# Gate and up of a SwiGLU layer: four of eight pairs of k-tiles as 2x2 blocks with seven products, and one shared set of large tiles

## Chip, cores and metric

The kernel runs on one core of a Trainium2 chip. The metric is the time of one execution on the device in microseconds, the median of three runs. Matrix products are TensorE's (PE), elementwise work is done by VectorE (DVE) and ScalarE (ACT), GpSimd (POOL) has a few small operations, and SyncE (SP) issues the loads.

## The reference

Two layers of a hybrid encoder over 256 positions with 2048 channels, all in float32. The part that the change touches is the last but one line of a layer:

```
for l in range(DEPTH):                                   # DEPTH = 2
    h = rmsnorm(x, norm1_g[l])
    proj = h @ w_in[l]                                   # q, k, v, uv
    a = dilated_attention(q, k, v)
    g = chunked_spatial_gating(uv, ...)
    x = x + concat(rmsnorm(a), rmsnorm(g)) @ w_out[l]
    h = rmsnorm(x, norm2_g[l])                           # 256 x 2048
    ff = silu(h @ w_gate[l]) * (h @ w_up[l])             # 2048 x 5632 each
    x = x + ff @ w_down[l]                               # 5632 x 2048
return rmsnorm(x, final_g)
```

## The kernel before

Every matrix product is made of three terms. A weight tile arrives as float32 ("raw"); ACT copies it to a shorter form ("hi", L646) and DVE subtracts that from the raw tile ("lo", L647). Activations are split in the same way. A product then takes three matmuls of 128x128 by 128x512 (TERMS, L699): hi by hi, hi by lo and lo by hi.

The weights come in 1 MB loads. One load is a **pair** of k-tiles (2 x 128 rows of the weight) by two column blocks of 512. A **group** (`_groups`) is one output of 256 rows by two such column blocks, so it fills four PSUM banks (two halves t of the rows, two blocks n). For gate and up, block n = 0 is 512 columns of gate and n = 1 the same 512 columns of up, and a group runs over 8 pairs: 8 x 24 = 192 matmuls. There are 11 such ff groups in a layer, in parts of FF_PARTS = (4, 4, 3); behind each part come two groups that apply the rows of w_down belonging to it.

When a group's last pair is done, ACT takes the gate banks (silu, L482), DVE multiplies them with the up banks (L485) into ffn, and a side task (`Ffn.turn`) transposes ffn on PE (tpf), and splits the result on ACT (L181) and DVE (L182) for the down groups.

The order is written by hand. One program loop goes over the pairs, in two **slots** of 12 matmuls each (t = 0, 1). In a slot it issues, in this order: the loads three pairs ahead (LA_DMA), the splits up to three slots ahead (LA_SPLIT), the slot's matmuls, the evacuations of banks that are complete (`done`), and up to two steps of side tasks (`run_side`). Each engine takes its own instructions strictly in the order in which they are issued, so an instruction that waits holds everything behind it on that engine. The tile pools have 4 raw, 4 hi and 4 lo tiles, PSUM has five banks for groups and three for side tasks.

Of the kernel before, what the change touches and what calls it, by code (L numbers as in the profile page):

```python
# [8 lines left out]
F32 = mybir.dt.float32  # L9
# [25 lines left out]
FF_PARTS = (4, 4, 3)  # L35
# [3 lines left out]
CH = 2 * NB  # L39
LA_DMA = 3  # L40
LA_SPLIT = 3
WARM = 4
TAIL = 2
# [10 lines left out]
def _groups():  # L54

    for l in range(DEPTH):
        seen = {}
        for what, ca, cb in W_IN:
            seen[what] = idx = seen.get(what, -1) + 1
            yield l, what, idx, 0, KD // 2, (("w_in", ca), ("w_in", cb))  # L60
        for what, row in (("oa", 0), ("og", DA)):
            for m in range(2):
                yield l, what, m, row, 4, (("w_out", 2 * m * NB), ("w_out", (2 * m + 1) * NB))
        j0 = 0
        for i, nj in enumerate(FF_PARTS):
            for m in range(j0, j0 + nj):
                yield l, "ff", m, 0, KD // 2, (("w_gate", m * NB), ("w_up", m * NB))
            for m in range(2):
                yield l, f"down{i}", m, j0 * NB, 2 * nj, (("w_down", 2 * m * NB), ("w_down", (2 * m + 1) * NB))
            j0 += nj  # L70


@with_exitstack
def encoder_kernel(ctx: ExitStack, tc: tile.TileContext, x, xf, w, ws, lng, cols, fg, cs, msk, out):
# [33 lines left out]
    mskt = cpool.tile([P, NT, SEQ], F32, name="mskt")  # L108

# [80 lines left out]

    def transposes(src, k, name):
# [14 lines left out]
    class Norm:  # L206


        def __init__(self, l, which):
            self.l, self.which = l, which  # L210
            self.ss = smp.tile([P, NT, D // NB], F32, tag="ssn", name=f"ssn_{which}_{l}", bufs=2)
            self.blocks = [KTiles(hpool, "h", f"h_{which}_{l}_{b}") for b in range(KD // KR)]
            self.n = 0
            self.rstd = None

# [10 lines left out]
        def block(self, b):  # L226

            for k in (0, 2):
                ps = transposes(xt[b], k, f"tpn_{self.which}_{self.l}_{b}_{k}")
                yield 1  # L230
                put_splits(self.blocks[b], k, ps, [gcol(self.l, self.which, b * KR + k + j) for j in range(2)])
# [3 lines left out]
        def early(self, b, k, src):  # L235

            put_split(self.blocks[b], k, src, gcol(self.l, self.which, b * KR + k))
# [11 lines left out]
        def lhs(self, k):  # L249
            force(lambda: self.blocks[k // KR].ready[k % KR])  # L250
            return self.blocks[k // KR], k % KR


    class Mixer:


        def __init__(self, l, norm):
# [9 lines left out]
            self.v = [None, None]  # L267
            self.u = [None, None]
# [3 lines left out]
        def load(self):  # L272
            l = self.l
            self.lng = s4p.tile([P, DG], F32, tag="s4", name=f"lng_{l}")
            self.ws = s4p.tile([P, NG, P], F32, tag="s4", name=f"ws_{l}")
# [4 lines left out]
        def value(self, t, half, ps):  # L280
            if self.v[half] is None:
                self.v[half] = mpool.tile([P, 2, NT, NB], F32R, tag="mf", name=f"v_{self.l}_{half}")
# [42 lines left out]
        def head(self, h):  # L325
# [11 lines left out]
            sm = s2p.tile([P, NT, SEQ], F32, tag="sm", name=f"sm_{l}_{h}")  # L337
# [22 lines left out]
            pT = s2p.tile([P, 2, NT, SEQ], F32R, tag="pT", name=f"pT_{l}_{h}")  # L360
# [4 lines left out]
            for c in range(NT):  # L365
                for n, (a, b) in enumerate(TERMS):
# [407 lines left out]
```

## Time and profile before

| | before |
|---|---|
| median of 3 runs | 2167.38 us (2167.27 to 2167.85) |
| profiled execution: its time | 2170.74 us |
| profiled execution: span from first to last instruction | 2168.9 us |
| mean granted TensorE clock | 0.997 |
| PE busy | 2138.9 us (99%) |
| DVE busy | 1169.3 us (54%) |
| ACT busy | 958.1 us (44%) |
| weight loads of 1 MB | 375 |

Busy time counts the instructions that compute, not waiting. A PE that is busy 99% of the span says only that it hardly ever waits; whether an engine with 54% has room at a certain place is read from a window, and how long its instructions take from their rows. All matmul rows print a duration of some 390 ns though they start 227 ns apart: they are pipelined, and the pace is the distance of their starts.

### The profile page before, as it was taken

The page shows a single profiled execution, that of the slowest core. Times are in us where ns is not written, and L with a number is a line of the kernel's source. Part 1 is how long each engine was busy: PE and PEld are TensorE (multiplying, and loading weights), DVE is VectorE, ACT ScalarE, POOL GpSimd, SP SyncE. Part 2 cuts the span into 40 slices and gives each one's busy share as a digit, 9 for nine tenths or more (in the row PEclk, how much of TensorE's full clock was granted, in tenths as well). Part 3 has the DMA queues.
Part 4 walks back from the last instruction along what each step waited for, and adds up shares of the span by engine and source line. Part 5 has one row for each costly group of instructions (what it writes and reads, how often), then busy time and mean ns, then how long its engine had stood idle before and what let it go on. Part 6 is the DMA issues. An engine that isn't in the chain of part 4 may idle for free.

```text
span 2168.9 us, 24017 instructions
## 1 busy us (share of the span) xinstructions
PE 2138.9 (99%) x9696; PEld 1770.0 (82%) x9696; DVE 1169.3 (54%) x1258; ACT 958.1 (44%) x1215; POOL 85.8 (4%) x64
## 2 busy tenths in 40 slices
PE   8999999999999999999999999999999999999997
PEld 6877888888888888888888788888888888888886
DVE  5577656445444444444556766554444454445445
ACT  5445545444334443344454555454433344333443
POOL 0121100000000000000002200000000000000000
PEclk9999999999999999999999999999999999999999
DMA  8444455555555555555555444555555555555552
GB/s 321 176 160 170 175 188 179 191 185 187 194 194 194 183 187 194 193 194 186 184 185 182 156 175 175 191 179 193 187 186 193 194 192 194 185 193 188 191 213 97
DMA packets 58800, 405.85 MB, mean 187 GB/s; under 512 B 6592, under 2 KB 6592, under 8 KB 10560
## 3 DMA queue, kind: packets, MB, share of 16 engines
q1 hardware_dynamic: 58688, 404.31, 51.9%
q8 instruction: 76, 1.25, 0.2%
q14 instruction: 36, 0.29, 0.0%
HBM read 402.19 MB, written 2.10 MB: 186 GB/s over the span
## 4 chain that ended last, share of the span: by engine, by line
PE 95%; DVE 2%; DMA 1%; issue 0%; ACT 0%; SPq 0%; POOL 0%; POOLq 0%; DVEq 0%; ACTq 0%
PE mm L699 92%; DVE lo L647 1%; PE tpf L196 1%; DVE rb_q L305 1%; DMA raw<-in_w 1%; PE sp L333 1%; PE op L367 1%; PE tpn_n L196 0%; DMA xf<-in_xf 0%; PE ptp L359 0%; PE mix L436 0%; DVE rb_k L305 0%; ACT hi L646 0%; PE tpg L196 0%; SPq L666 0%
## 5 line engine op out<-in xcount | busy, mean ns | idle before, releaser
L647 DVE TENSOR_TENSOR lo<-raw,hi 128x1024 fp32r<-128x1024 f32 (+1 forms) x754 | 904.5, 1226 | 930.9 <-ACT hi L646 928.4
L699 PE MATMUL mm<-hi,h_n 128*128 128x512 f32 x4096 | 1291.1, 392 | 7.9 <-ACT hi L646 5.0
L646 ACT ACTIVATE hi<-raw 128x1024 fp32r<-128x1024 f32 (+1 forms) x754 | 767.8, 1051 | 1050.9 <-PE mm L699 1028.5
L699 PEld LDWEIGHTS mm<-hi,h_n 128*128 128x128 f32 x4096 | 771.0, 188 | 167.6 <-ACT hi L646 6.2
L699 PE MATMUL mm<-lo,h_n 128*128 128x512 f32 x2048 | 800.7, 391 | 7.8 <-DVE lo L647 7.8
L699 PEld LDWEIGHTS mm<-lo,h_n 128*128 128x128 f32 x2048 | 385.8, 188 | 89.1 <-DVE lo L647 12.6
L699 PE MATMUL mm<-hi,ff 128*128 128x512 f32 x1408 | 438.9, 390 | 0.0
L699 PEld LDWEIGHTS mm<-hi,ff 128*128 128x128 f32 x1408 | 264.3, 188 | 54.6
L699 PE MATMUL mm<-lo,ff 128*128 128x512 f32 x704 | 274.0, 389 | 0.0
L699 PEld LDWEIGHTS mm<-lo,ff 128*128 128x128 f32 x704 | 132.2, 188 | 27.0
L699 PE MATMUL mm<-hi,a 128*128 128x512 f32 x256 | 84.1, 399 | 0.0
L699 PE MATMUL mm<-hi,g 128*128 128x512 f32 x256 | 81.3, 392 | 0.0
L699 PEld LDWEIGHTS mm<-hi,a 128*128 128x128 f32 x256 | 48.1, 188 | 10.0
L699 PEld LDWEIGHTS mm<-hi,g 128*128 128x128 f32 x256 | 48.1, 188 | 9.8
L699 PE MATMUL mm<-lo,a 128*128 128x512 f32 x128 | 49.9, 390 | 0.0
L699 PE MATMUL mm<-lo,g 128*128 128x512 f32 x128 | 49.9, 390 | 0.0
L203 POOL TENSOR_TENSOR rstd_n<-rstd_n,mhalf 128x2 f32<-128x2 f32 x4 | 2.8, 696 | 926.2 <-DVE rstd_n L202 926.2
L181 ACT ACTIVATE ff<-tpf 128x512 fp32r<-128x512 f32 x44 | 26.4, 600 | 29.0 <-PE tpf L196 27.6
L182 DVE TENSOR_TENSOR ff<-tpf,ff 128x512 fp32r<-128x512 f32 x44 | 30.2, 687 | 7.9 <-ACT ff L181 7.9
L485 DVE SCALAR_TENSOR_TENSOR ffn<-mm,rstd_n,sil 128x512 f32<-128x512 f32 x44 | 32.9, 747 | 1.6 <-ACT sil L482 1.3
L602 DVE TENSOR_TENSOR xt<-mm,xt 128x512 f32<-128x512 f32 x48 | 30.9, 681 | 4.0 <-PE mm L699 4.0
L346 ACT ACTIVATE sm<-sm,mx 128x256 f32<-128x256 f32 x32 | 16.0, 502 | 37.9 <-DVE mx L343 37.9
(103 smaller groups left out, 708.0 us busy)
## 6 DMA issues: line engine op xcount, KB each, us to landing
raw<-in_w SPq DMA_DIRECT2D x375, 1024.0 KB, 4.8
xt<-in_x SPq DMA_DIRECT2D x4, 512.0 KB, 13.6
out<-xt SPq DMA_DIRECT2D x8, 256.0 KB, 3.1
xf<-in_xf SPq DMA_DIRECT2D x3, 512.0 KB, 10.2
raw<-in_w SPq DMA_DIRECT2D x4, 256.0 KB, 6.5
ws<-in_ws SPq DMA_DIRECT2D x2, 512.0 KB, 3.6
lng<-in_lng SPq DMA_DIRECT2D x2, 512.0 KB, 5.4
fg<-in_fg SPq DMA_DIRECT2D x1, 1024.0 KB, 7.0
```

The lines of the kernel that those rows point to most:

```text
L181: nc.scalar.activation(out=hi, in_=src, func=AF.Copy)
L182: nc.vector.tensor_tensor(out=kt.t[:, k:k + 2, 1, :], in0=src, in1=hi.bitcast(F32), op=ALU.subtract)
L196: nc.tensor.transpose(ps[:, j, t, :], src[:, t, (k + j) * P:(k + j + 1) * P], ident)
L305: nc.vector.tensor_tensor(out=b[:, :, to], in0=s[:, :, of], in1=sin, op=ALU.mult)
L333: nc.tensor.matmul(sp[:, t, :], lhsT=q[:, a, i, t * P:(t + 1) * P], rhs=k[:, b, i, :], start=(n == 0), stop=(n == len(TERMS) - 1),)
L346: nc.scalar.activation(out=sm[:, t, :], in_=sm[:, t, :], func=AF.Exp, bias=mx[:, t:t + 1], accum_out=den[:, t:t + 1])
L367: nc.tensor.matmul(op, lhsT=v[:, a, c, f * HD:(f + 1) * HD], rhs=pT[:, b, c, :], start=(c == 0 and n == 0), stop=(c == NT - 1 and n == len ...
L485: nc.vector.scalar_tensor_tensor(out=self.ff[:, t, :], in0=ps, scalar=self.norm.scale(t), in1=self.silu, op0=ALU.mult, op1=ALU.mult)
L602: nc.vector.tensor_tensor(out=xb, in0=ps, in1=xb, op=ALU.add)
L646: nc.scalar.activation(out=hi[:, sl], in_=src[:, sl], func=AF.Copy)
L647: nc.vector.tensor_tensor(out=lo[:, sl], in0=src[:, sl], in1=hi[:, sl].bitcast(F32), op=ALU.subtract)
L699: nc.tensor.matmul(ps, lhsT=a.part(xl, ka, t), rhs=hl[kk][wl][:, n, :], start=(j == 0 and kk == 0 and z == 0), stop=(j == pairs - 1 and kk ...
```

## The change

The ff groups change their arithmetic. The first four of the eight pairs of a group ("fast") are taken as 2x2 blocks: A11 to A22 are the two row halves of the activations by the two k-tiles of a pair, B11 to B22 the two k-tiles by gate and up. Seven products give the four results (Strassen's scheme in Winograd's form). Each product M1 to M7 runs over the four fast pairs with three terms: 12 matmuls, one slot, into a bank. The weights' sums (T1 to T4) are made by DVE in place in the raw tiles q11, q12, q21, q22 of 128x2048 (`add`, L836), between the splits that need the earlier contents; the activations' sums (S1 to S4) are made once for a layer by `sums` (L252, L255, L256) when norm2's result is there. The other four pairs stay as they were, in two slots each. A group has 15 slots instead of 16, in the order of ORDER, or of FIRST for the first ff group of a layer.

Splits in ff groups are made of 2048 columns at once (L858 on ACT, L859 on DVE). M1 and M5 go to banks that ACT copies to SBUF (L913); DVE adds the products together (`finish`, L917 to L927) and silu (L623) and the multiplication (L626) read the SBUF sums. FF_PARTS becomes (3, 3, 3, 2). The separate pools of raw, hi, lo and other large tiles give way to one shared set of 17 tiles of 8 KB in each partition (`Big`). Loads are issued five slots ahead, splits two slots ahead in ff groups with an index above 0 and three elsewhere. The transposes for norm2 start earlier: `delay=1 + n, rank=0` instead of `delay=1 + 4 * n`.

```diff
-FF_PARTS = (4, 4, 3)
-CH = 2 * NB
-LA_DMA = 3
+FF_PARTS = (3, 3, 3, 2)
+FAST = {"ff": 4}
+BANK = {(0, 0): "v", (0, 1): "z", (1, 0): "x", (1, 1): "w"}
+PRODUCT = {
+    "M1": ("1", "A11", "B11"), "M2": ("v", "A12", "B21"), "M3": ("z", "S4", "B22"), "M4": ("x", "A22", "T4"),
+    "M5": ("5", "S1", "T1"), "M6": ("6", "S2", "T2"), "M7": ("7", "S3", "T3"),
+}
+ORDER = ("N", "M1", "N", "M5", "M2", "N", "M6", "M3", "M7", "M4", "N")
+FIRST = ("M1", "M5", "M2", "M6", "M3", "N", "M7", "N", "M4", "N", "N")
+LOADS = {"M1": ("q11", "q12"), "M5": ("q22",), "M2": ("q21",)}
+CH = 4 * NB
+N_BIG = 17
+LA_LOAD = 5
 LA_SPLIT = 3
...
+    def sums(raw, n, dst):
+        r = raw.view("p (j f q) -> p j f q", j=2, f=8)[:, :n]
+        f = lambda i: r[:, :, i, :]
+        for to, a, op, b in (
+            (3, f(7), ALU.subtract, f(2)), (4, f(3), ALU.subtract, f(0)),
+            (5, f(0), ALU.subtract, f(7)), (6, f(1), ALU.add, f(4)),
+        ):
+            nc.vector.tensor_tensor(out=f(to), in0=a, in1=b, op=op)
+        src = r[:, :, 0:7, :].rearrange("p j f q -> p j (f q)")
+        hi, lo = (dst.rearrange("p (j h z) -> p j h z", h=2, z=7 * P)[:, :, i] for i in range(2))
+        nc.scalar.activation(out=hi, in_=src, func=AF.Copy)
+        nc.vector.tensor_tensor(out=lo, in0=src, in1=hi.bitcast(F32), op=ALU.subtract)
...
             if what == "og" and t == NT - 1:
-                spawn(norms["n2", l].block(b), delay=1 + 4 * n)
+                spawn(norms["n2", l].block(b), delay=1 + n, rank=0)
...
+        def add(self, to, of):
+            cols = self.fast * NB
+            a, b = (self.raw[q].t[:, :cols] for q in (to, of))
+            nc.vector.tensor_tensor(out=a, in0=a, in1=b, op=ALU.add)
...
+        def split(self, key, pieces=1):
...
+                q = {"M1": "q11", "M5": "q11", "M6": "q11", "M2": "q21", "M4": "q21", "M7": "q12", "M3": "q22"}
...
+            if key == "M3":
+                self.add("q12", "q22")
...
+                nc.scalar.activation(out=hi[:, sl], in_=src[:, sl], func=AF.Copy)
+                nc.vector.tensor_tensor(out=lo[:, sl], in0=src[:, sl], in1=hi[:, sl].bitcast(F32), op=ALU.subtract)
...
+            if key == "M1":
+                self.add("q11", "q12")
+            elif key == "M5":
+                self.add("q11", "q22")
+            elif key == "M2":
+                self.add("q21", "q11")
...
+                b, f, _ = PRODUCT[m]
+                for p in range(self.fast):
+                    act = norms["n2", self.l].form(p)
+                    for z, (xl, wl) in enumerate(TERMS):
+                        mac(b, act(xl, f), hl[0][wl][:, p * NB:(p + 1) * NB],
+                            self.last[b] == i and p == self.fast - 1 and z == len(TERMS) - 1)
...
+        def finish(self, b):
+            ps, c = self.banks[b][0], self.copies
+            if b in "15":
+                c[b] = sx(f"m{b}_{self.g}")
+                nc.scalar.activation(out=c[b], in_=ps, func=AF.Copy)
+                return
+            if b == "6":
+                c["x"] = sx(f"m16_{self.g}")
+                nc.vector.tensor_tensor(out=c["x"], in0=ps, in1=c["1"], op=ALU.add)
+                c["z"] = sx(f"m5_16_{self.g}")
+                nc.vector.tensor_tensor(out=c["z"], in0=c["5"], in1=c["x"], op=ALU.subtract)
+                return
+            if b == "7":
+                nc.vector.tensor_tensor(out=c["x"], in0=ps, in1=c["x"], op=ALU.add)
+                nc.vector.tensor_tensor(out=c["5"], in0=c["5"], in1=c["x"], op=ALU.subtract)
+                c["v"], c["w"] = c["1"], c["5"]
+                return
+            if b in c:
+                nc.vector.tensor_tensor(out=c[b], in0=ps, in1=c[b], op=ALU.add)
+                ps = c[b]
+            t, n = next(k for k, v in BANK.items() if v == b)
+            done(self.l, self.what, self.idx, t, n, ps)
...
+    events = sorted(
+        [(s - LA_LOAD, 0, i) for i, (s, *_) in enumerate(loads) if i >= KD // KR]
+        + [(s - (2 if gr.fast and gr.idx else LA_SPLIT), 1, i) for i, (s, gr, _) in enumerate(splits)]
+    )
```

What stands in the engines' queues is told by the program, without times. The names are made of the group's number (9 is the first ff group of layer 0, 20 one in its third part) and the product or pair, and the last number only counts.

ACT's queue before, around the silu of an ff group (here gate block 8 of layer 0, group 21):

```order
L646 ACTIVATE hi_320_6567<-raw_160_6515 128x1024
L646 ACTIVATE hi_321_6585<-raw_160_6515 128x1024
L482 ACTIVATE sil_0_8_0_6596<-mm_21_0_0_6347,rstd_n2_0_2992 128x512
L646 ACTIVATE hi_322_6605<-raw_161_6549 128x1024
L482 ACTIVATE sil_0_8_1_6615<-mm_21_1_0_6365,rstd_n2_0_2992 128x512
L646 ACTIVATE hi_323_6627<-raw_161_6549 128x1024
```

ACT's queue after the change, at the start of group 20 (layer 0), behind the second silu of the group ahead:

```order
L623 ACTIVATE sil_0_6_1_5486<-m16_19_5398,rstd_n2_0_2816 128x512
L858 ACTIVATE hi_20_M1_5498<-raw_20_q11_5439 128x2048
L858 ACTIVATE hi_20_5_5519<-raw_20_5_5455 128x2048
L913 ACTIVATE m1_20_5552<-mm_20_1_5539 128x512
L858 ACTIVATE hi_20_M5_5554<-raw_20_q11_5439 128x2048
L858 ACTIVATE hi_20_M2_5572<-raw_20_q21_5517 128x2048
L234 ACTIVATE ff_0_6_5571<-tpf_0_6_0_5589 128x2x256
L858 ACTIVATE hi_20_6_5596<-raw_20_6_5537 128x2048
```

Before, only the silu stands between the splits of weights. After, the copy of M1's bank (m1) stands between hi 5 and hi M5, so everything behind it comes after M1's matmuls.

DVE's queue after the change, at the same place; q11, q12, q21, q22 are the raw tiles of the weight blocks:

```order
L927 TENSOR_TENSOR m5_19_5332<-mm_19_w_5251,m5_19_5332 128x512
L626 SCALAR_TENSOR_TENSOR ffn_0_6_5468<-m5_19_5332,rstd_n2_0_2816,sil_0_6_1_5486 128x512
L859 TENSOR_TENSOR lo_20_M1_5499<-raw_20_q11_5439,hi_20_M1_5498 128x2048
L836 TENSOR_TENSOR raw_20_q11_5439<-raw_20_q11_5439,raw_20_q12_5441 128x2048
L859 TENSOR_TENSOR lo_20_5_5520<-raw_20_5_5455,hi_20_5_5519 128x2048
L859 TENSOR_TENSOR lo_20_M5_5555<-raw_20_q11_5439,hi_20_M5_5554 128x2048
L836 TENSOR_TENSOR raw_20_q11_5439<-raw_20_q11_5439,raw_20_q22_5496 128x2048
L859 TENSOR_TENSOR lo_20_M2_5573<-raw_20_q21_5517,hi_20_M2_5572 128x2048
L836 TENSOR_TENSOR raw_20_q21_5517<-raw_20_q21_5517,raw_20_q11_5439 128x2048
L235 TENSOR_TENSOR ff_0_6_5571<-tpf_0_6_0_5589,ff_0_6_5571 128x2x256
L859 TENSOR_TENSOR lo_20_6_5597<-raw_20_6_5537,hi_20_6_5596 128x2048
```

Where the queue before has one lo part of 1024 columns for each slot, here lo parts and additions of 2048 columns alternate, and the lo part of pair 6, which PE needs in its eighth slot, stands behind four lo parts and three additions of its group.

DVE's queue after the change in the first ff group of layer 0; hr and h_n2 are the activations' sums and their split, xt the residual, to which L757 adds the product of w_out:

```order
L836 TENSOR_TENSOR raw_9_q11_2538<-raw_9_q11_2538,raw_9_q12_2540 128x2048
L252 TENSOR_TENSOR hr_n2_0_1_2513<-hr_n2_0_1_2513 128x2x128 x4
L256 TENSOR_TENSOR h_n2_0_2330<-hr_n2_0_1_2513,h_n2_0_2330 128x2x896
L859 TENSOR_TENSOR lo_9_M5_2619<-raw_9_q11_2538,hi_9_M5_2618 128x2048
L836 TENSOR_TENSOR raw_9_q11_2538<-raw_9_q11_2538,raw_9_q22_2567 128x2048
L757 SCALAR_TENSOR_TENSOR xt_2_99<-mm_8_v_2469,rstd_g_0_2290,xt_2_99 128x512
L757 SCALAR_TENSOR_TENSOR xt_3_100<-mm_8_z_2470,rstd_g_0_2290,xt_3_100 128x512
L859 TENSOR_TENSOR lo_9_M2_2642<-raw_9_q21_2589,hi_9_M2_2641 128x2048
L836 TENSOR_TENSOR raw_9_q21_2589<-raw_9_q21_2589,raw_9_q11_2538 128x2048
L757 SCALAR_TENSOR_TENSOR xt_2_99<-mm_8_x_2497,rstd_g_0_2290,xt_2_99 128x512
```

PE's queue at the same place, between M1 and M5 of that group:

```order
L880 MATMUL mm_9_1_2666<-hi_9_M1_2591,h_n2_0_2330 128x512 x2
L880 MATMUL mm_9_1_2666<-lo_9_M1_2592,h_n2_0_2330 128x512
L880 MATMUL mm_9_1_2666<-hi_9_M1_2591,h_n2_0_2330 128x512
L264 MATMUL tpn_n2_0_4_2681<-ident_81,xt_2_99 128x128 x4
L880 MATMUL mm_9_5_2691<-hi_9_M5_2618,h_n2_0_2330 128x512
L880 MATMUL mm_9_5_2691<-lo_9_M5_2619,h_n2_0_2330 128x512
```

The last addition into xt_2 stands behind two further lo parts and two block additions on DVE, and PE's transposes of xt_2 stand ahead of M5.

## Rows read from the trace of the kernel before

**Rows 1.** The page: span, busy time, chain that ended last, weight loads.

```profile
span 2168.9 us, 24017 instructions
...
PE 2138.9 (99%) x9696; PEld 1770.0 (82%) x9696; DVE 1169.3 (54%) x1258; ACT 958.1 (44%) x1215; POOL 85.8 (4%) x64
...
PE 95%; DVE 2%; DMA 1%; issue 0%; ACT 0%; SPq 0%; POOL 0%; POOLq 0%; DVEq 0%; ACTq 0%
...
raw<-in_w SPq DMA_DIRECT2D x375, 1024.0 KB, 4.8
```

**Rows 2.** Waits of PE: us in total, times, longest us.

```profile
PE mm L699 <- DVE lo L647: 7.8, 8, 1.3
```

**Rows 3.** Four ff groups: us; busy PE, PEld, DVE, ACT, POOL; PEclk; DMA; GB/s.

```profile
353.52:531.00 177.48, 177.48 (x804) 146.97 (x803) 89.85 (x91) 80.86 (x100) 0.69 (x1) 1.00 0.53 189
```

**Rows 4.** Timeline of PE in the ff groups: start us, us, operation.

```profile
443.18 0.62 PE L699 MATMUL mm<-hi,h_n 128*128 128x512 f32 x2
...
443.86 0.62 PE L699 MATMUL mm<-hi,h_n 128*128 128x512 f32 x2
...
446.13 0.60 PE L196 MATMUL tpf<-ident,ffn 128*128 128x128 f32 x4
...
490.60 0.60 PE L196 MATMUL tpf<-ident,ffn 128*128 128x128 f32 x4
```

**Rows 5.** Tiles hi and lo: duration ns min/median/max, first and last start.

```profile
L646 ACT ACTIVATE hi<-raw x754: 629/1058/1101, 7.1 to 2145.4; 128x1024 fp32r<-128x1024 f32 x188, 128x512 fp32r<-128x512 f32 x1
L647 DVE TENSOR_TENSOR lo<-raw,hi x754: 691/1224/2314, 7.8 to 2146.7; 128x1024 fp32r<-128x1024 f32 x188, 128x512 fp32r<-128x512 f32 x1
```

**Rows 6.** Timelines of DVE and ACT at four places.

```profile
715.98 0.68 DVE L182 TENSOR_TENSOR ff<-tpf,ff 128x512 fp32r<-128x512 f32 x1
716.58 1.21 DVE L647 TENSOR_TENSOR lo<-raw,hi 128x1024 fp32r<-128x1024 f32 x1
...
742.51 2.36 DVE L647 TENSOR_TENSOR lo<-raw,hi 128x1024 fp32r<-128x1024 f32 x2 [3.08 <-ACT hi L646]
...
741.42 2.01 ACT L646 ACTIVATE hi<-raw 128x1024 fp32r<-128x1024 f32 x2 [3.43 <-PE mm L699]
...
196.87 0.68 DVE L338 SCALAR_TENSOR_TENSOR sm<-sp,mskt 128x512 f32<-128x512 f32 x1
197.59 0.69 DVE L343 TENSOR_REDUCE mx<-sm 128x2 f32<-128x512 f32 x1
```

**Rows 7.** Groups of instructions: busy us, mean ns of one, idle before them.

```profile
L699 PE MATMUL mm<-hi,h_n 128*128 128x512 f32 x4096 | 1291.1, 392 | 7.9 <-ACT hi L646 5.0 <-ACT s_q L293 2.9
L482 ACT ACTIVATE sil<-mm,rstd_n 128x512 f32<-128x512 f32 x44 | 29.9, 679 | 0.6
L181 ACT ACTIVATE ff<-tpf 128x512 fp32r<-128x512 f32 x44 | 26.4, 600 | 29.0 <-PE tpf L196 27.6
L598 DVE SCALAR_TENSOR_TENSOR xt<-mm,rstd_g,xt 128x512 f32<-128x512 f32 x16 | 11.2, 743 | 0.0
L172 DVE SCALAR_TENSOR_TENSOR h_n<-tpn_n,colt,h_n 128x256 fp32r<-128x256 f32 x48 | 20.9, 476 | 0.0
```

**Rows 8.** Timeline of PE at the start.

```profile
7.83 0.80 PE L699 MATMUL mm<-hi,h_n 128*128 128x512 f32 x1 [4.40 <-ACT hi L646]
...
11.66 1.05 PE L699 MATMUL mm<-hi,h_n 128*128 128x512 f32 x2
12.52 0.63 PE L699 MATMUL mm<-lo,h_n 128*128 128x512 f32 x1
...
15.29 0.63 PE L699 MATMUL mm<-hi,h_n 128*128 128x512 f32 x2
```

**Rows 9.** Timeline of PE around a set of norm2's transposes.

```profile
350.34 0.60 PE L196 MATMUL tpn_n<-ident,xt 128*128 128x128 f32 x4
350.69 0.48 PE L699 MATMUL mm<-hi,g 128*128 128x512 f32 x1
```

**Rows 10.** Cores: span and mean granted TensorE clock.

```profile
core 0: 2168.9 us, clock 0.997
```

More of the change, by code (lines that the diff above doesn't have):

```diff
@@ L247, in scale, with normal, form @@
             return self.rstd[:, t:t + 1]
-        def lhs(self, k):
-            force(lambda: self.blocks[k // KR].ready[k % KR])
-            return self.blocks[k // KR], k % KR
+        def normal(self, p):
+            force(lambda: self.ready[p])
+            return lambda hl, kk, t: self.pairs[p].part(hl, kk, t)
+        def form(self, p):
+            force(lambda: self.ready[p])
+            return lambda hl, f: self.pairs[p][:, hl, FORMS[f], :]
     class Mixer:
@@ L457, in gating @@
                 return
+            for z in (self.gvb, self.lw, self.ub):
+                z.free()
             yield 1
@@ new lines, in encoder_kernel @@
+    groups = [Group(g, spec) for g, spec in enumerate(_groups())]
+    slots, loads, first_slot = [], [], {}
+    off = 0
+    for gr in groups:
+        first_slot[gr.g] = len(slots)
+        for key, width, i in gr.loads():
+            loads.append((first_slot[gr.g] + i, gr, key, width, off))
+            off += P * width
+        slots += [(gr, i) for i in range(len(gr.slots))]
+    splits, seen = [], set()
+    for s, (gr, i) in enumerate(slots):
+        for key in gr.chunks(gr.slots[i]):
+            if (gr.g, key) not in seen:
+                seen.add((gr.g, key))
+                splits.append((s, gr, key))
@@ new lines, in encoder_kernel, with next_event @@
+    events = sorted(
+        [(s - LA_LOAD, 0, i) for i, (s, *_) in enumerate(loads) if i >= KD // KR]
+        + [(s - (2 if gr.fast and gr.idx else LA_SPLIT), 1, i) for i, (s, gr, _) in enumerate(splits)]
+    )
+    pos = 0
+    def next_event(now, must):
+        nonlocal pos
+        if pos == len(events):
+            return False
+        when, kind, i = events[pos]
+        due = splits[i][0] if kind else loads[i][0]
+        if not must:
+            need = splits[i][1].need(splits[i][2]) if kind else 1
+            if count["live"] + need > N_BIG - reserve(now) or when > now:
+                return False
+        if kind:
+            _, gr, key = splits[i]
+            gr.split(key, pieces=2 if i < 2 else 1)
+        else:
+            _, gr, key, width, o = loads[i]
+            gr.load(key, width, o)
+        pos += 1
+        return True
@@ new lines, in reserve, with split_by @@
+    def reserve(now):
+        gr = slots[now][0]
+        return {"v": 1, "qk": 2, "gv": 1, "u": 1, "oa": 1, "og": 1, "ff": 1}.get(gr.what, 1)
+    def split_by(s):
+        while pos < len(events) and any(
+            (splits[i][0] if kind else loads[i][0]) <= s for _, kind, i in events[pos:pos + 12]
+        ):
+            assert next_event(s, True)
+    xf_b = [Big(f"xf_{b}") for b in range(2)]
+    xf_t = [xf_b[b // 2].view("p (b k q) -> p b k q", b=2, k=KR)[:, b % 2] for b in range(KD // KR)]
```

411 lines of the change are left out of this document (287 added, 124 removed).

## Prediction

> **What bounds the kernel now.** I read the head of the page first. TensorE (PE) is busy 99% of the span and 95% of the chain that ended last; VectorE (DVE) has 54% and ScalarE (ACT) 44% [rows 1]. The view of waits agrees: PE's longest sum of waits is 7.8 us for lo parts, in 8 waits of the whole span [rows 2]. In the first four feed-forward (ff) groups PE is busy 177.48 of 177.48 us while DVE works 89.85 and ACT 80.86 [rows 3]: half of DVE's time is free there. The timeline gives PE's pace: three matmuls in 0.68 us, 0.2267 each; the same transposes return after 490.60 - 446.13 = 44.47 us, which is one ff group: 192 matmuls (43.52) and 0.95 for its transposes [rows 4]. So what counts is whether the other engines can still feed PE once a group has fewer matmuls and more vector work.
>
> **What is removed.** A group in blocks has 180 matmuls: 15 slots of 12, each 2.72 us, so 40.80 + 0.95 = 41.75 us instead of 44.47. With 22 ff groups that is 264 x 0.2267 = 59.8 us, all on the path that sets the end, if nothing else comes up.
>
> **What is added on DVE and ACT.** Durations first. A lo part of 1024 columns takes 1.224 us and one of 512 takes 0.691, so 0.533 for each 512 more [rows 5]; back to back the second 1024 starts some 1.14 after the first, and an operation behind one of 512 starts 0.60 after it [rows 6]. For 2048 columns, which no row of before has, I estimate 2.29 us long and 2.20 from start to start; an addition of the same size reads and writes the same amounts, so it gets the same. Bounds: 2 x 1.22 = 2.44 above (nothing gained by the longer form) and 4 x 0.533 = 2.13 below (no fixed part). An operation that needs the result of the one just ahead starts 0.04 after its end instead of 0.09 before it [rows 6]. A hi part on ACT goes 0.629, 1.058, so 1.92 for 2048 [rows 5]. Additions of 512 columns cost 0.68 to 0.69 [rows 6], silu 0.68 and a copy of a bank on ACT 0.60 [rows 7]. A bank's sum is out 0.392 - 0.227 = 0.165 after the last matmul's turn [rows 4, 7]; with the hand-over I take 0.2, and 0.05 for other hand-overs, as between ACT's 741.42 + 1.06 and DVE's 742.51 [rows 6].
>
> Splits per group: before 16 of 1024 columns (18.2 us of DVE), now eleven of 2048, and four additions of 2048 (the sums of weight blocks): 15 x 2.20 = 33.0. About twelve operations of 512 (recombination, activation, transposed results) give 7.3, and seven waits for its own result 0.9: 41.2 us of DVE for 41.75 us of PE. That alone leaves 0.5 us of slack; the order of the queues takes it away. ACT has some 26 us of work and room.
>
> **A steady ff group** (7 of 11 in a layer), t = 0 at the end of the group before on PE. ACT's queue there reads silu, hi M1, hi 5, the copy of M1's bank, hi M5, hi M2. The silu ends at 0.28, hi M1 at 2.1, and DVE does lo M1 2.15 to 4.44, the addition q11 += q12 4.48 to 6.77, lo 5 6.68 to 8.97. Pair 5 is due in PE's fourth slot at 8.16, so PE stalls 0.86. hi M5's input has been there since 6.77, but ahead of it on ACT stands the copy, which waits for M1, the third slot (ends at 8.16 plus 0.2): copy 8.36 to 8.96, hi M5 8.9 to 10.8. Behind that queue lo M5 10.85 to 13.14 (DVE idle for 1.9 us), q11 += q22 to 15.47, lo M2 15.38 to 17.67, q21 += q11 17.71 to 20.00, one transposed result to 20.60, lo 6 20.51 to 22.80. Pair 6 is due in PE's eighth slot at 9.02 + 4 x 2.72 + 0.95 = 20.85 and starts at 22.85: a stall of 2.0. The eight slots from there are covered by 0.7 to 1.5 us each, so the group ends at 22.85 + 21.76 = **44.61**, 0.14 more than before. The matmuls saved (2.72) come back as two stalls (2.86).
>
> **The three groups behind a down part** have no silu ahead and no transposes within: lo 6 ends at 22.20, the eighth slot starts at 22.25 and the group ends at 44.01, where 43.52 stood: +0.49.
>
> **The first group** (FIRST) has its block sums M1, M5, M2, M6, M3 ahead, which are three products and four additions of DVE work with little PE work between. With U its start: lo M1 and q11 += q12 are done at 0, then four small sums of the second activation block (L252, 0.48 or less each, as L172 [rows 7]) to 1.65, ACT's 1792 columns to 3.4, its lo to 5.4; M1 ends at 6.35, not 2.72. DVE goes on: lo M5 to 7.5, q11 += q22 to 9.9, two additions into xt (L757, 0.74 as L598 [rows 7]) to 11.2, lo M2 to 13.4, q21 += q11 to 15.7, and only then the xt addition for x to 16.45. PE's queue has the transposes of that block (tpn, xt_2) behind M1 and ahead of M5, so M5, whose parts have lain ready since 7.5, starts at 16.9: PE idles some 10 us. Then it runs by its own pace and ends at U + 56.0, of which the four extra sets of transposes (0.35 each, 350.34 to 350.69 [rows 9]) also stood in the kernel before: 54.6 against 43.52, +11.1. After this idle time the clock may fall. The only such row is at the start: after 4.40 us of idle PE's matmuls come 0.43 apart (12.52 - 11.66 for two), the half-speed level of 1.2 GHz, from 7.83 to 14.2; by 15.29 two take 0.63 where one takes 0.39, so 0.24 apart [rows 7, 8]. The mean granted clock of the span, 0.997 [rows 10], fits that: 0.003 x 2168.9 = 6.5 us short of full, or 13 us at half. That makes 3.2 us lost; the lower end is nothing, since PE was barely used ahead of that row. I take 3.2, as 10 us of idle is more than 4.4. The first group: +14.3.
>
> On that clock, the Trainium skill (TensorE: Matmul & The Clock Gate, "Part 1: The HAM clock gate") says that the array runs at half rate after an idle spell and returns after a spell of sustained work. The row at the start agrees with it.
>
> **The last down part** has two ff blocks (FF_PARTS ends in 2), so the transposes of the last block come right ahead of the matmuls that need them: transpose, ACT 0.60, DVE 0.69 [rows 6, 7] with no other matmuls under them, 1.3 twice: +2.6. Everything else is covered: loads stay at 1 MB with 4.8 us to landing [rows 1] and are issued five slots (13.6 us) ahead; without that cover a late one would cost at most those 4.8.
>
> **The sum.** Per layer 7 x 0.14 + 3 x 0.49 + 14.3 + 2.6 = 19.4, twice 38.8 us. The profiled execution took 2170.74 (span 2168.9), so 2209.5; the median of the runs lies 3.36 below that profiled one, so **2206 us**, 1.8% slower.
>
> **The rivals.** (1) PE stays the bound. Should the 2048-wide operations pass in 1.9 us or less, the two stalls of a steady group vanish (2.86 over the nine large operations up to lo 6) and 20 groups save 2.72 each, -54.4; the first group and the last down part still cost 2 x 16.9: 2147. Were the first group not held either, 2108. Against it: 1.9 is below the lower bound of 2.13. For it: DVE's idle 1.9 us behind the copy on ACT is worked out from an order, and some 0.9 us less there would already halve the loss. (2) Gain and cost meet: lo 6 earlier by 1.5 us in 20 groups takes 30 us off: 2176, and with an undisturbed clock 2170. (3) Dearer: 2048-wide operations at the upper bound of 2.44 cost nine times 0.24 more in each of 20 groups, +43: 2249. Milder: no overlap between them, next.
>
> For two DVE operations in a row the 1024-wide pair takes 2.36 us where two alone take 2.45, so the second starts before the first ends [rows 6]. The Trainium skill (VectorE: DVE Perf Modes, "The DRAIN you can't avoid") says that the next operation doesn't start until the pipe has emptied. By it each large step would be 2.29 instead of 2.20, six of them unheld up to lo 6: +0.55 a group, 11 us in all, 2217. The row speaks against it, and the sum keeps 2.20.
>
> **How the numbers follow.** The forecast with its own range 2178 to 2222 (clock undisturbed and 2.13-wide steps below; no overlap, and a little dearer, above) gets 0.70. The rival in which PE stays the bound (2108 to 2165) gets 0.14, the meeting of both (2165 to 2178) 0.08, the dearer one (above 2222) 0.08. Leaving out the first and the last of these gives a range of 2168 to 2222 that holds some 0.78. A measurement of this kernel can tell about 0.2%, 4.3 us, from no change: faster 0.17, the same 0.04, slower 0.79.
>
> **What would show it.** In the profile after: L880 with idle time put down to DVE lo, twice in each steady group, ahead of pairs 5 and 6; a lo part of 2048 columns at 2.29; hi M5 on ACT right behind the copy of M1's bank with DVE idle before lo M5; DVE busy near 1660 us; a gap of some 10 us on PE ahead of M5 in the first ff group of both layers, with matmuls 0.43 apart after it. It would be wrong if PE shows no idle time in the steady groups (a transposed pair returns after 41.75), if the large operations pass in 1.9, or if the gap in the first group is short because DVE reached the xt additions earlier.

## The result and the profile after

The changed kernel takes 2192.83 us (median of 4 runs, 2191.24 to 2195.05) against 2167.49 for the kernel before: 1.0117 times as long, 95% interval 1.010 to 1.0135. It is slower by 25.3 us, where 38.8 were forecast. The page of its profile, its cores and PE's longest waits (us in total, times, longest) answer to [rows 1], [rows 10] and [rows 2]:

```profile
PE 2098.2 (96%) x9432; PEld 1720.2 (79%) x9432; DVE 1619.8 (74%) x1432; ACT 1072.1 (49%) x1153; POOL 79.4 (4%) x64
...
PE 80%; DVE 11%; issue 6%; ACT 3%; DMA 0%; SPq 0%; DVEq 0%; POOLq 0%; POOL 0%; ACTq 0%
...
core 0: 2190.0 us, clock 0.992
...
PE mm_v L880 <- DVE lo L859: 38.8, 34, 1.6
PE tpn_n L264 <- DVE xt L757: 18.7, 4, 5.4
PE mm_v L880 <- DVE lo_M L859: 5.8, 6, 1.0
```

The 264 matmuls are gone (9432 instead of 9696), and PE's busy time fell by 40.7 us. But DVE now has 11% of the chain, and PE waits 38.8 us for lo parts. The number of these waits is that of the forecast: 34 is two in each of the 14 steady groups and one in each of the 6 behind a down part. The last row, lo M2 in those 6 groups, was not forecast. DVE is busy 1619.8 us, where near 1660 was forecast.

**A steady group.** DVE, ACT and PE at the start of the second ff group (start us, us, operation; in brackets the idle time before it and what ended it):

```profile
406.41 2.29 DVE L859 TENSOR_TENSOR lo_M<-raw_q,hi_M 128x2048 fp32r<-128x2048 f32 x1 [1.05 <-ACT hi_M L858]
408.74 2.29 DVE L836 TENSOR_TENSOR raw_q<-raw_q,raw_q 128x2048 f32<-128x2048 f32 x1
410.94 2.28 DVE L859 TENSOR_TENSOR lo<-raw,hi 128x2048 fp32r<-128x2048 f32 x1
414.30 2.29 DVE L859 TENSOR_TENSOR lo_M<-raw_q,hi_M 128x2048 fp32r<-128x2048 f32 x1 [1.07 <-ACT hi_M L858]
...
423.97 2.28 DVE L859 TENSOR_TENSOR lo<-raw,hi 128x2048 fp32r<-128x2048 f32 x1
...
411.87 0.60 ACT L913 ACTIVATE m<-mm 128x512 f32<-128x512 f32 x1 [3.69 <-PE mm L880]
412.37 3.71 ACT L858 ACTIVATE hi_M<-raw_q 128x2048 fp32r<-128x2048 f32 x2
...
411.67 0.39 PE L880 MATMUL mm_v<-hi,hb_n 128*128 128x512 f32 x1
413.28 0.50 PE L880 MATMUL mm_v<-lo,hb_n 128*128 128x512 f32 x1 [1.22 <-DVE lo L859]
...
426.30 0.50 PE L880 MATMUL mm_v<-lo,hb_n 128*128 128x512 f32 x1 [0.90 <-DVE lo L859]
```

The large operations take 2.29 us and follow each other after 2.20, as estimated from rows of half the size. ACT is idle for 3.69 us ahead of the copy of M1's bank (411.87), and hi M5 comes right behind the copy at 412.37, though q11 += q12 was done at 411.03; DVE then waits 1.07 us for it. PE starts pair 5's first matmul at 411.67 and stands 1.22 us for its lo part, and pair 6's 0.90 us. In the groups that follow it is the other way round, some 0.6 and 1.5 (2.1 in all). The same transposes come back after 44.52 us, which answers to the 44.47 of [rows 4]:

```profile
617.02 0.60 PE L264 MATMUL tpf<-ident,ffn 128*128 128x128 f32 x4
...
661.54 0.60 PE L264 MATMUL tpf<-ident,ffn 128*128 128x128 f32 x4
...
447.99:492.47 44.48, 42.36 (x189) 34.42 (x188) 41.39 (x28) 25.13 (x20) 0.00 (x0) 1.00 0.45 160
```

The last line is the window of the third group (stretch, us, busy PE, PEld, DVE, ACT, POOL, PEclk, DMA, GB/s), which answers to [rows 3]: DVE is busy 41.39 of 44.48 us, where before it was busy half the time.

**The first group.** DVE and PE from ahead of M1 to M5 of layer 0, then two windows with the same columns:

```profile
342.79 2.29 DVE L836 TENSOR_TENSOR raw_q<-raw_q,raw_q 128x2048 f32<-128x2048 f32 x1
...
354.78 0.75 DVE L757 SCALAR_TENSOR_TENSOR xt<-mm_v,rstd_g,xt 128x512 f32<-128x512 f32 x1
...
356.10 2.28 DVE L859 TENSOR_TENSOR lo_M<-raw_q,hi_M 128x2048 fp32r<-128x2048 f32 x1
358.42 2.29 DVE L836 TENSOR_TENSOR raw_q<-raw_q,raw_q 128x2048 f32<-128x2048 f32 x1
360.63 0.74 DVE L757 SCALAR_TENSOR_TENSOR xt<-mm_x,rstd_g,xt 128x512 f32<-128x512 f32 x1
...
347.55 0.39 PE L880 MATMUL mm<-hi_M,h_n 128*128 128x512 f32 x1
...
355.58 0.47 PE L264 MATMUL tpn_n<-ident,xt 128*128 128x128 f32 x1 [3.98 <-DVE xt L757]
361.43 0.90 PE L264 MATMUL tpn_n<-ident,xt 128*128 128x128 f32 x3 [5.37 <-DVE xt L757]
...
352.00:362.00 10.00, 1.04 (x5) 0.76 (x5) 9.93 (x9) 5.44 (x4) 0.00 (x0) 0.52 0.00 0
362.00:367.00 5.00, 5.00 (x17) 3.95 (x16) 5.00 (x4) 0.07 (x1) 0.00 (x0) 0.59 0.30 95
```

PE waits 3.98 + 5.37 = 9.35 us for additions into xt while DVE is busy 9.93 of 10 us with the blocks' work. In both stretches the granted clock is 0.52 and 0.59, so near the level of 1.2 GHz; M5's twelve matmuls take from 361.98 to 366.73, 4.75 us instead of 2.72; most of them come 0.43 apart, as forecast.

### The profile page after: what moved, and what is told of

Read it like the earlier page. It is cut to its first block, busy times and chain, and to the rows that moved or that the text cites. A ratio compares the mean times of both kernels' runs of the same rounds, so it can differ in the third digit from the quotient of the medians.

```text
span 2190.0 us, 23316 instructions
## 1 busy us (share of the span) xinstructions
PE 2098.2 (96%) x9432; PEld 1720.2 (79%) x9432; DVE 1619.8 (74%) x1432; ACT 1072.1 (49%) x1153; POOL 79.4 (4%) x64
## 4 chain that ended last, share of the span: by engine, by line
PE 80%; DVE 11%; issue 6%; ACT 3%; DMA 0%; SPq 0%; DVEq 0%; POOLq 0%; POOL 0%; ACTq 0%
PE mm_z L880 18%; PE mm_x L880 18%; PE mm_v L880 16%; PE mm_w L880 16%; PE mm L880 8%; DVE lo_M L859 5%; DVE lo L859 2%; ACT hi_M L858 2%; DVE hl L859 1%; PE sp L449 1%; DVE raw_q L836 1%; DVE rb_k L419 0%; PE op L489 0%; PE tpn_n L264 0%; DVE ff L235 0%
## 5 line engine op out<-in xcount | busy, mean ns | idle before, releaser
L859 DVE TENSOR_TENSOR hl<-raw,hl 128x1024 fp32r<-128x1024 f32 (+1 forms) x402 | 479.3, 1240 | 74.4 <-ACT hl L858 72.7
L858 ACT ACTIVATE hl<-raw 128x1024 fp32r<-128x1024 f32 (+1 forms) x402 | 399.9, 1048 | 124.6 <-PE mm_w L880 83.4
L859 DVE TENSOR_TENSOR lo_M<-raw_q,hi_M 128x2048 fp32r<-128x2048 f32 x154 | 350.4, 2286 | 51.0 <-ACT hi_M L858 51.0
L858 ACT ACTIVATE hi_M<-raw_q 128x2048 fp32r<-128x2048 f32 x154 | 288.1, 1909 | 131.3 <-DVE raw_q L836 111.2
L880 PE MATMUL mm<-hi_M,h_n 128*128 128x512 f32 x704 | 236.5, 397 | 1.7 <-DVE h_n L256 1.7
L859 DVE TENSOR_TENSOR lo<-raw,hi 128x2048 fp32r<-128x2048 f32 x88 | 200.7, 2285 | 32.1 <-ACT hi L858 21.9
L836 DVE TENSOR_TENSOR raw_q<-raw_q,raw_q 128x2048 f32<-128x2048 f32 x88 | 201.6, 2290 | 2.3
L858 ACT ACTIVATE hi<-raw 128x2048 fp32r<-128x2048 f32 x88 | 167.6, 1908 | 49.9 <-PE mm_w L880 43.0
L880 PE MATMUL mm_v<-hl,ff 128*128 128x512 f32 x528 | 136.2, 392 | 2.7 <-ACT ff L234 2.7
L880 PE MATMUL mm<-lo_M,h_n 128*128 128x512 f32 x352 | 138.8, 394 | 0.0
```

The costliest lines, as they stand in the source:

```text
L836: nc.vector.tensor_tensor(out=a, in0=a, in1=b, op=ALU.add)
L858: nc.scalar.activation(out=hi[:, sl], in_=src[:, sl], func=AF.Copy)
L859: nc.vector.tensor_tensor(out=lo[:, sl], in0=src[:, sl], in1=hi[:, sl].bitcast(F32), op=ALU.subtract)
L880: nc.tensor.matmul(bank[0], lhsT=lhsT, rhs=rhs, start=bank[1], stop=stop)
```

## The experiments

My theory: the order of the queues (the copy ahead of hi M5 on ACT, block additions ahead of the xt additions on DVE) turns the saved matmuls into waits. The rivals: DVE's amount of work sets the pace whatever the order, or the shared tiles and the other parts cost the time. All runs below are against the kernel before, 2167.5 to 2168.2 us.

| run | median us | ratio to before, 95% interval |
|---|---|---|
| e1_no_blocks | 2169.18 | 1.0005 [0.9995, 1.0014] |
| e2_late_copy | 2151.37 | 0.9922 [0.9907, 0.9936] |
| e3_first_two_ahead | 2185.82 | 1.0082 [1.0067, 1.0097] |
| e4_no_adds | 2120.80 | 0.9785 [0.9768, 0.9801] |
| e5_pool_add | 2263.19 | 1.0437 [1.0422, 1.0453] |
| e6_first_order | 2160.33 | 0.9961 [0.9946, 0.9976] |
| e7_parts_443 | 2166.50 | 0.9992 [0.9983, 1.0002] |
| e8_all | 2255.76 | 1.0409 [1.0393, 1.0424] |
| e9_first_two | 2145.82 | 0.9896 [0.9881, 0.9911] |
| e10_hi_early | 2140.95 | 0.9874 [0.9859, 0.9889] |
| e11_both | 2138.73 | 0.9853 [0.9836, 0.9870] |
| e12_add_later | 2138.87 | 0.9865 [0.9848, 0.9881] |

**e1_no_blocks.** No block products; the shared tiles, the look-ahead of the loads, the parts and the early transposes of the change are kept. The weights are then split 1024 columns at a time and three slots ahead, as in the kernel before.

```diff
-FAST = {"ff": 4}
+FAST = {}
```

> All eight pairs of the ff groups in the plain way (no block products), but with the shared set of large tiles, the longer look-ahead of the loads and FF_PARTS = (3, 3, 3, 2). If the loss lies in the blocks alone: PE is the bound again, the projections ahead of attention keep the 8.2 us that they gained in the changed kernel (6.0 and 2.2 in the two layers), and the last down part of each layer costs its 2.4: 2167.5 - 8.2 + 4.9 = 2164 us. Rival: the shared tiles cost or gain by themselves in the ff groups too; then the pitch of an ff group differs from 44.47, and 22 of them move the time by more than 5 us from 2164.

Measured 2169.18, 1.6 above before and 5 above the expectation. The ff part of a layer is 2.5 us longer (348.50 to 1083.27 in the trace, 734.77 us, against 732.28), as the shorter last part makes it; the pitch of an ff group (the distance from a row to the same row one group later) stays 44.5 (a part of three takes 132.45). So the shared tiles cost nothing in the ff groups, and the loss of 25 lies in the blocks, with their splits and additions of 2048 columns. Blocks with splits of 1024 columns were not tried. The gain ahead of attention is smaller than the 8.2 read from the two profiled executions: by the medians it is 2 x 2.5 - 1.6 = 3.4. The profiled execution of the kernel before was itself 3.4 us above its median: from 100 to 200 us its granted clock was 0.98, and 1.00 in the changed kernel.

**e2_late_copy.** The copy of M1's bank is issued one slot later.

```diff
         def finish(self, b):
             ps, c = self.banks[b][0], self.copies
+            if b == "1" and self.idx:
+                self.late = b
+                return
...
```

What is not printed makes `run()` issue the copy behind the next slot's matmuls.

> Only the copy of M1's bank on ACT comes one slot later, behind hi M5 (all ff groups but the first of a layer). If the order of ACT's queue holds back DVE's chain: hi M5 starts with the end of q11 += q12, lo M5 to lo 6 come 1.9 us earlier, the second stall of a steady group (1.2 us lost on average) and most of that in the groups behind a down part (1.5) go: 14 x 1.2 + 6 x 1.5 = 26 us less, 2167 us. Rival: DVE's work (some 41.5 us of a group's 44.5) sets the pace whatever the order, the stall moves to a later slot and the time stays within 5 us of 2193.

Measured 2151.37, 41.5 less than the changed kernel and now faster than before. ACT, DVE and PE's waits of this run:

```profile
412.87 1.92 ACT L859 ACTIVATE hi_M<-raw_q 128x2048 fp32r<-128x2048 f32 x1 [2.94 <-DVE raw_q L837]
414.69 0.58 ACT L915 ACTIVATE m<-mm 128x512 f32<-128x512 f32 x1
...
412.70 2.28 DVE L860 TENSOR_TENSOR lo<-raw,hi 128x2048 fp32r<-128x2048 f32 x1
414.90 2.28 DVE L860 TENSOR_TENSOR lo_M<-raw_q,hi_M 128x2048 fp32r<-128x2048 f32 x1
...
PE tpn_n L264 <- DVE xt L757: 18.7, 4, 5.4
PE mm_v L882 <- DVE lo L860: 9.3, 14, 1.2
...
612.71 0.60 PE L264 MATMUL tpf<-ident,ffn 128*128 128x128 f32 x4
...
655.40 0.60 PE L264 MATMUL tpf<-ident,ffn 128*128 128x128 f32 x4
```

hi M5 now waits for its own input only, lo M5 follows lo 5 without a gap, and 34 waits for lo (38.8 us) became 14 (9.3). The pitch of a steady group is 42.69. The rival of a full DVE falls as the explanation of the loss. The gain is larger than the 26 expected. I had counted only the waits that the view prints, but a stall of PE costs some 0.3 more around it (in the changed kernel 44.50 - 41.75 = 2.75 for two stalls printed as 2.11), and the lo M2 behind a down part (5.8 us in six waits) went too.

**e3_first_two_ahead.** The first group of a layer with a look-ahead of two slots.

```diff
-        + [(s - (2 if gr.fast and gr.idx else LA_SPLIT), 1, i) for i, (s, gr, _) in enumerate(splits)]
+        + [(s - (2 if gr.fast else LA_SPLIT), 1, i) for i, (s, gr, _) in enumerate(splits)]
```

> Only the look-ahead of the splits in the first ff group of a layer is two slots instead of three, so that the last additions into xt stand ahead of lo M2 and q21 += q11 on DVE. If PE waits there for these additions behind DVE's queue: they come some 4 us earlier, M1 starts at most 0.5 later, less time at the lower clock: 4 to 5 us in each layer, 2184 us. Rival: the stall is DVE's total work ahead of M3, so what is saved ahead of M5 is lost again ahead of M6 and M3: 2191 to 2195.

Measured 2185.82, 7.0 less than the changed kernel. PE's wait for the xt additions goes from 9.35 to 6.26 us in each layer. The queue ahead of these additions costs, as expected.

```profile
359.53 0.90 PE L264 MATMUL tpn_n<-ident,xt 128*128 128x128 f32 x3 [6.26 <-DVE xt L757]
```

**e4_no_adds.** `add` returns at once.

> The four additions of weight blocks (2048 columns, 2.29 us each) are left out in every ff group, so M4 to M7 multiply unsummed weights. Both theories expect that no steady group waits: 20 groups at 41.75 instead of 44.5 and 43.9, -53, and the first group shorter by the two additions ahead of the xt addition and the clock, -6 each: 2193 - 65 = 2128 us. If it stays above 2160, neither the additions nor the queue behind them is the cause, and PE's stalls have another one (loads, banks).

Measured 2120.80, 72 less than the changed kernel. A part of three groups takes 124.30 us (545.88 to 670.18): 40.80 for the one behind the down part, which has no transposes, and 41.75 for each of the others, the 40.80 + 0.95 of the forecast. That is a group's time with nothing in PE's way. The expectation gave the six groups behind a down part 41.75 as well, which is 5.7 of the 7 us by which it was too high. As the weights' sums are left out, the run shows times only.

**e5_pool_add.** On top of e2.

```diff
-            nc.vector.tensor_tensor(out=a, in0=a, in1=b, op=ALU.add)
+            (nc.gpsimd if to == "q12" else nc.vector).tensor_tensor(out=a, in0=a, in1=b, op=ALU.add)
```

> On top of the late copy: one of the four additions of weight blocks (q12 += q22) moves from DVE to GpSimd. If DVE's own work is what is left of the steady groups' bound (one stall of 0.67 us, with its restart some 0.8, in 14 groups): DVE loses 2.2 us of work a group and the stall goes, 11 us less, 2140 us. Rival: GpSimd takes long over 2048 columns (512 took 1.5 to 2.2 us before, so 6 to 9) or holds DVE up at the shared memory; then the product M7 waits and the time is the same as with the late copy, 2151, or more.

Measured 2263.19, 112 more than e2. GpSimd in the first ff group, then GpSimd and DVE in the second:

```profile
346.93 4.57 POOL L837 TENSOR_TENSOR raw_q<-raw_q,raw_q 128x2048 f32<-128x2048 f32 x1 [53.54 <-DVE raw_q L837]
...
417.13 6.54 POOL L837 TENSOR_TENSOR raw_q<-raw_q,raw_q 128x2048 f32<-128x2048 f32 x1 [27.42 <-DVE raw_q L837]
...
416.92 2.28 DVE L860 TENSOR_TENSOR lo<-raw,hi 128x2048 fp32r<-128x2048 f32 x1
419.12 6.70 DVE L860 TENSOR_TENSOR lo_M<-raw_q,hi_M 128x2048 fp32r<-128x2048 f32 x1
```

The lo part that starts while GpSimd adds takes 6.70 us instead of 2.29 and ends 2.15 us after GpSimd's end at 423.67: it stood until then. GpSimd stood as well: the addition takes 4.57 us in the first group, and 6.54 here, where it starts under lo 5 and 4.47 us are left of it from that part's end at 419.20. The rival was right in that DVE is held up; it is not M7 that waits for it but M5, M2 and pair 6. The Trainium skill (SBUF — State Buffer, "Who interferes with whom") says that a DVE instruction with two inputs in SBUF contends with a GpSimd instruction that reads SBUF, and that the port pair which they share is an exclusive lock. The trace agrees: moving 2.2 us of DVE's work cost DVE 4.4, in each of the 20 groups behind the first of a layer. The mean granted clock also fell, from 0.990 to 0.982; what that took of the 112 us was not separated.

**e6_first_order** and **e9_first_two**, both on top of e2: two other orders of the first group.

```diff
-FIRST = ("M1", "M5", "M2", "M6", "M3", "N", "M7", "N", "M4", "N", "N")
+FIRST = ("M1", "N", "N", "M5", "M2", "N", "M6", "M3", "M7", "M4", "N")    # e6
+FIRST = ("M1", "M5", "N", "M2", "M6", "N", "M3", "M7", "N", "M4", "N")    # e9
...
```

Both also shorten the look-ahead in this group and put one addition later, as the expectations say.

> On top of the late copy: the first ff group of a layer takes its plain pairs 4 and 5 right behind M1, and q11 += q12 and the splits of the other products come later, so that the additions into xt have one lo part ahead of them, not three products' work. If PE's gap there is DVE's queue: the gap of 9.4 us shrinks to about 3 and the clock stays up (2 us), 8 us in each layer, 2135 us. Rival: the blocks' DVE work is only put off and PE waits for M5 to M3 later in that group: less than 4 us in each layer, 2144 or more.

> On top of the late copy, only the first ff group of a layer: order M1, M5, N, M2, M6, N, M3, M7, N, M4, N; M5's split one slot ahead and the others two, so that all four additions into xt stand ahead of lo M5; q11 += q22 moves behind lo M2. Against the other order tried, M5 lies between the transposes of pair 4 and its matmuls. If PE's gap is DVE's queue ahead of the xt additions and the work can be spread between plain pairs: the group goes from 56 to 47 us, 9 us in each layer, 2134 us. Rival: the parts of pair 4 are late again (transpose, ACT, DVE in a row with PE idle) and the clock falls all the same: at most 4 us in each layer, 2143 or more.

e6 measured 2160.33, 9 more than e2; e9 2145.82, 5.6 less. In both the time is that of the rival, but the waits are mostly others than it named. PE in e6, then its longest waits in e9 and the windows behind them:

```profile
366.08 0.80 PE L885 MATMUL mm_v<-hi,hb_n 128*128 128x512 f32 x1 [3.14 <-ACT hb_n L223]
370.76 1.22 PE L885 MATMUL mm_v<-hi,hb_n 128*128 128x512 f32 x2 [3.46 <-DVE hb_n L225]
...
PE mm L885 <- DVE lo_M L860: 8.0, 4, 2.1
...
353.36 0.55 PE L264 MATMUL tpn_n<-ident,xt 128*128 128x128 f32 x3 [0.98 <-DVE xt L757]
...
356.22 0.80 PE L885 MATMUL mm<-lo_M,h_n 128*128 128x512 f32 x1 [2.08 <-DVE lo_M L860]
...
350.00:355.00 5.00, 3.13 (x14) 1.93 (x13) 5.00 (x6) 3.64 (x3) 0.00 (x0) 0.98 0.00 0
355.00:360.00 5.00, 3.78 (x9) 3.01 (x10) 3.36 (x2) 0.55 (x2) 0.00 (x0) 0.50 0.00 0
```

In e6 the gap for the xt additions shrinks from 9.35 to 1.5 us, but the transposed parts of pairs 4 and 5 (hb) then come one after the other with PE waiting for each; the rival had M5 to M3 wait. In e9 two waits of 2 us are left in each layer, for lo M5 and lo M6 and not for pair 4, which waits 0.4. The clock falls all the same: it is 0.50 behind the first of them, though PE was busy 3.13 of the 5 us ahead. The work is only partly spread.

**e7_parts_443.** On top of e2: FF_PARTS = (4, 4, 3).

> On top of the late copy: FF_PARTS = (4, 4, 3) as in the kernel before. If the last down part of two blocks costs its 2.4 us because its transposes come right ahead of their matmuls, that goes in both layers: 2151 - 5 = 2146 us. Rival: with four blocks the shared set of 17 tiles runs short, loads or splits come late and the time is 2151 or more.

Measured 2166.50, 15 more than e2. The last down part does shrink (its ff blocks are there earlier), but PE's waits for lo are 20 instead of 14 and 19.6 us in all, and four for lo M2 (5.6 us) are new. The long ones stand in the fourth group of a part, 1.39 for lo M2 and 2.11 for pair 6. ACT takes hi M2 there behind a transposed result that it waits 5.75 us for, while in the third group hi M2 comes right behind the copy of M1's bank:

```profile
PE mm_v L882 <- DVE lo L860: 19.6, 20, 2.1
...
PE mm_v L882 <- DVE lo_M L860: 5.6, 4, 1.4
...
505.88 0.60 ACT L234 ACTIVATE ff<-tpf 128x512 fp32r<-128x512 f32 x1 [5.75 <-PE tpf L264]
506.38 1.91 ACT L859 ACTIVATE hi_M<-raw_q 128x2048 fp32r<-128x2048 f32 x1
```

The program puts a split off (`next_event`) when the shared set has too few free tiles, so this order fits the rival; a larger set was not tried.

**e10_hi_early** and **e11_both.** hi M1 is issued ahead of the second silu of the group before; e11 has e9's first group too. (A combination of the late copy, the GpSimd addition, e6's order and FF_PARTS (4, 4, 3), labelled e8_all and expected at 2119, measured 2255.76. It holds the GpSimd addition that cost 112 us in e5; its parts were not taken apart.)

```diff
...
+        if gr.fast and i == len(gr.slots) - 1 and groups[gr.g + 1].fast:
+            groups[gr.g + 1].hi_early()
         gr.run(i)
```

> On top of the late copy, in the groups that follow another ff group: hi M1 on ACT comes ahead of the second silu of the group before. If what is left in a steady group (0.6 us of waiting with 0.15 behind it) comes from the 1.05 us in which DVE waits for hi M1: lo M1 starts up to 0.65 earlier and the wait goes, 14 x 0.8 = 11 us less, 2140 us. Rival: DVE is full in that group (42.0 us) and the wait moves to another slot, or the silu comes later and holds lo M1 as before: 2149 to 2153.

> Late copy, the new order of the first group and the early hi M1 together. If each removes a wait of its own: 2151 - 17 - 11 = 2123 us. If one of the two fails alone, the time is that of the other.

e10 measured 2140.95, 10.4 less than e2, as expected: the waits for lo in steady groups are all but gone, and the pitch is 650.88 - 608.83 = 42.05, 0.3 from the 41.75 of a PE that never waits.

```profile
PE mm_v L888 <- DVE lo L866: 0.7, 2, 0.3
...
608.83 0.60 PE L264 MATMUL tpf<-ident,ffn 128*128 128x128 f32 x4
...
650.88 0.60 PE L264 MATMUL tpf<-ident,ffn 128*128 128x128 f32 x4
```

e11 measured 2138.73 (2132.15 to 2139.79), 12.6 less than e2, where the two alone sum to 16: not told apart from the sum within the spread of its runs, of which the one at 2132.15 had a mean granted clock of 0.997 and the others 0.992 to 0.993. The 2123 expected counted 17 us for e9's order, and 5.6 came.

**e12_add_later.** On top of e11: in the first group q21 += q11 goes behind lo M6.

> On top of all three (late copy, new order of the first group, early hi M1): in the first group q21 += q11 moves behind lo M6. If the second gap there (1.93 us, followed by matmuls at half pace) is that addition ahead of lo M6 on DVE: the gap goes, and with it 1.2 us of lower clock, some 3 us in each layer, 2133 us. Rival: hi M6, which waits for q11 += q22 in any case, sets the gap and the clock falls as before: 2137 to 2140.

Measured 2138.87, no change: the rival's time, but not its wait. The wait at M6 fell from 1.9 to 0.90 us, and a new one of 2.17 stands at pair 5:

```profile
373.29 0.50 PE L895 MATMUL mm<-lo_M,h_n 128*128 128x512 f32 x1 [0.90 <-DVE lo_M L866]
...
378.47 0.50 PE L895 MATMUL mm_v<-lo,hb_n 128*128 128x512 f32 x1 [2.17 <-DVE lo L866]
```

Moving one addition only moves the wait. This suggests that in the first group, unlike the steady ones, the amount of work on DVE and ACT is what is left. e4 agrees: without the additions its first group waits 3.7 us in all.

## Why the prediction came out as it did

**Right, with the sum too large.** The direction and the mechanisms held: 2192.8 lies in the range and the time moved 25.3 us of the 38.8. By the stages of the two traces:

- *The saved matmuls* are worth what was said: 2.72 a group (e4: 41.75).
- *A steady group*: 44.61 forecast, 44.52 measured. The two stalls are ahead of pairs 5 and 6 as worked out. That the sizes agree so closely is partly luck: the stalls print 2.1 us, not 2.86, and the rest is the 0.3 around each, which I had not counted. That hi M5 behind the copy of M1's bank causes most of it is shown by e2, where only that order changed.
- *Behind a down part*: 44.01 forecast, 43.9 measured, in two waits (lo M2 0.96, pair 6 1.50) instead of one of 3.2.
- *The first group*: +14.3 forecast, +11.0 measured (347.55 to 403.51 is 55.96, against 43.52 and 1.4 for transposes). The step that was mis-sized: I put the end at U + 56.0 and then 3.2 for the clock on top, while 55.96 holds the clock's 2.0. That the ends agree is chance. DVE had q11 += q12 done at 345.08, 2.5 us ahead of U = 347.55, where I put it at U. So the xt addition ended at U + 13.8, not 16.45, PE's gap was 9.35 and not 10 or more, and M5 started 2.5 us earlier than forecast; the clock then took 2.0 of that back. The term is 3.3 us too large in each layer, 6.5 of the 13.5 us between forecast and result. e3, e6 and e9 show that the queue ahead of these additions makes the gap.
- *The last down part*: +2.6 forecast, +2.4 measured: 48.80 us for eight pairs, 5.28 beyond their matmuls, where before twelve took 68.12, 2.84 beyond.
- *Not in the sum at all*: the projections ahead of attention became shorter, 3.4 us by e1, more in the two profiled executions. I costed the shared tiles and the longer look-ahead there at nothing. That left 3.4 of the 13.5 us. What in them gained was not tried apart.

The steady groups, the groups behind a down part and the last down part give 2 to 3 us more. What is left is the uncertainty of setting one profiled execution against medians: mine took 3.36 off, and the profiled execution of the changed kernel lies 1.0 below its median.

**The rivals.** That PE stays the bound did not come, since a large operation took 2.20 and not 1.9, but its remark on the 0.9 us behind the copy named the weak point of the change: with the copy one slot later the kernel is 0.8% faster than before, with hi M1 earlier 1.3%. The dearer rivals fell: three lo parts in a row took 6.69 us in the changed kernel (2 x 2.20 + 2.29), so large operations overlap as the small ones do. The sum by which an operation starts only when the pipe is empty would have been 0.09 a step too long. The section of the Trainium skill that the prediction cites for it (VectorE: DVE Perf Modes, "The DRAIN you can't avoid") goes on that a next operation that is not held starts earlier. The 6.69 us agree with that.

```profile
386.01 6.69 DVE L859 TENSOR_TENSOR lo<-raw,hi 128x2048 fp32r<-128x2048 f32 x3
```

Three counts in the rivals were off, without effect on the forecast. Up to lo 6 the queue has eight large operations, not nine: the dearer rival costs 38 us and not 43, and the stalls vanish at 1.84 us and not 1.9. Three of these and one small operation are unheld, not six, so without overlap 7 us would be added and not 11. And 2108 drops the last down part's cost too; with only the first group not held, the same terms give 2113.

## What to carry to other kernels

Fewer matmuls pay only if the engines that feed them keep up instruction by instruction: DVE at 41.4 of 44.5 us had nearly no room, and one 0.6 us copy at the wrong place in ACT's queue cost more than 40 us over the kernel. Look in the order for an instruction that waits for late work (here a PSUM evacuation) with earlier-ready work behind it, and issue it after that work. Before moving DVE's work to GpSimd, see whether both read SBUF there.

## What the runs showed of the hardware

- A 128x2048 addition on GpSimd took 4.57 us in the two first groups, twice DVE's 2.29, and 6.37 to 6.55 in the 20 groups where it started under a DVE operation that reads two SBUF tiles. The DVE operation behind it stood until the addition had ended (6.70 us instead of 2.29).
- TensorE's granted clock was 0.50 behind waits of 0.98 and 2.08 us with PE busy for 3.13 of 5 us (e9). I had expected it only after a gap of several us without work.
- A DVE operation on 2048 columns takes 2.29 us, on 1024 columns 1.22: the fixed part is only some 0.16 us, so the larger tiles gained DVE little.
